# State space stage of a two-layer encoder step: scans of 512 columns instead of 128, and output products in fp32 over 128 rows

## The chip, the core and the metric

The kernel runs on one core of a Trainium2 chip. A core has five engines that each follow their own instruction order: TensorE (PE in the profile, with its weight loads as PEld), VectorE (DVE), ScalarE (ACT), GpSimd (POOL) and SyncE (SP, which here only issues DMAs). The metric is the device time of one execution in microseconds. Three runs of the kernel before gave 2142.64, 2145.76 and 2148.68 us, so the median is 2145.76 us.

## The reference

The program is one streaming step of a small encoder with two layers. Layer 0 mixes the sequence with a diagonal complex state space model (S5), layer 1 with a gated delta rule. Both are evaluated for a prompt of 2048 positions and for 8 short samples of 16 positions. The change touches layer 0 alone, and there the recurrence:

```python
# per group g of 16 channels, 64 complex states p
x_t = Abar * x_{t-1} + Bbar @ u_t          # complex, one decay per (g, p)
y_t = Re(C @ x_t)
y   = gelu(y + d * u);  y = y * sigmoid(y @ w_glu + b_glu) * silu(z)
out = y @ w_out
```

with `u, z = split(h @ w_in)`. The states after the last position are outputs too, of the prompt (`s5_re_prompt`, `s5_im_prompt`) and of the samples.

## The kernel before

Eight positions form one column. The 2048 prompt positions are 256 columns (`NPC`), the samples' 128 positions another 16, so every tile of the first layer has 272 columns (`NCH`). Layer 0 goes through three stages:

- Stage A computes the left half `u` of the input projection (`pd`), stores it, and builds tables: powers of `Abar` and the scaled `B` and `C` for 16 steps (`sp_d`), and rotation tables (`tw_d`).
- Stage B runs the state space model in 16 steps of four groups each (`s5_setup`, `s5_load`, `s5_main`). Between these instructions PE computes the right half `z` of the projection in 64 blocks (`z_block`, product `pdz`, 24 matmuls a block): each weight and activation is split into a high and a low part, and three products are summed (lines 150 to 152). The z blocks are written last in the program and have no deadline, so the scheduler takes them as filler for PE; only the last six carry an order (`later([ends...])`): they stand behind the output products of step 15.
- Stage C does the gate (`pg`, with `w_glu`) and the output projection (`po`, with `w_out`). Its weights come in blocks of 512 KB through two buffers (`wr`, pool `wrc`): DMA into `wgr` or `wor`, a cast on ACT into the high part (`wgh`, `woh`, L136), a subtraction on DVE for the low part (`wgl`, `wol`, L138). Eight blocks of `w_glu` are followed by eight of `w_out` and eight blocks `w2q` of the second layer.

One S5 step on its engines. Setup, one step ahead: four DVE products and a sum give `abt`, PE transposes it to `ab` (L679); four DVE products (L685, L686) and a difference (L687) give `ca`, which ACT and DVE split into a high and a low part (`cah`, `cal`, L130 and L131); PE makes the short-range kernel `pk` from it (L695), which goes through DRAM and comes back as `toe`. Main part: PE multiplies `u` by `ab` for the two pairs of groups, into `pb` (L732; PSUM has one buffer for it); ACT copies the sample columns (`bs`, L735); DVE rotates the prompt columns by the table (`f`, L737), adds and subtracts (`z`, L739 and L740), and scans: 256 columns in two segments of 128, for two pairs and for real and imaginary part apart, so eight scans of 128 columns (L746). Between the two segments four small DVE instructions (L750 to L753) rotate the end of the first into the start of the second. Two products rotate back (`t`, L760), a difference and a sum give the states `x` (named `xs` in the trace, L762 and L763). The 128 rows are two groups of 64 states. `x` is split into high and low parts (`xsh` on ACT, `xsl` on DVE). For each of four groups PE then sums `toe` times `u` in fp32 (L772) and six products over 64 rows (L777: real and imaginary part, each high by high, high by low, low by high), two groups side by side in the rows of the array. ACT applies gelu (L781), and the result goes to DRAM (`y_d`).

What sets the order: apart from the first part of stage A, which is written out by hand, the framework's scheduler fixes the instruction order of each engine when the program is built. On the chip each engine follows that order. SP and ACT issue the DMAs in their order as well, so a DMA that waits holds up the ones behind it. After its last loads for step 15, SP stores the samples' states (`s5s`, L800) and the prompt's states (`s5p`, L796), then loads the blocks of `w_glu` (L134), the outputs `y` (`yc`, L892) and `z` (`zt`, L931).

Beside DVE's last steps, POOL computes the samples' final states: eight tensor operations from L797 on, among them those of `advance`.

## Time and profile before

| | |
|---|---|
| median of three runs | 2145.76 us (2142.64 to 2148.68) |
| the profiled execution, its own time | 2142.89 us |
| its span, first to last instruction | 2141.1 us |
| busy in the span | PE 97%, DVE 73%, ACT 45%, POOL 23% |
| stage B, from the first `pdz` to the last | 270.7 to 617.8 us |
| mean granted PE clock | 0.989 |

The profile lists, for one execution, when every instruction started and how long it took. PE's matmuls are pipelined: one of 272 columns takes 0.29 us from start to end, but the next can start 0.13 us after it. An fp32 matmul stands in the trace as two records. A chain row names what set the time at that moment; a wait row names who waited for whom, the sum in us, how often, and the longest.

### The profile page before, as it was taken

What the parts mean: (1) busy time and instruction counts of PE and PEld (TensorE: products, weight loads), DVE (VectorE), ACT (ScalarE), POOL (GpSimd) and SP (SyncE); (2) the same over time, 40 slices, a digit from 0 to 9 for tenths busy, and PEclk for the clock granted to TensorE, in tenths of its full rate; (3) what the DMA queues carried; (4) which work ended last, traced back from release to release, by engine and by line L of the source; (5) the groups of instructions that cost most, each with busy time, mean ns of one, the idle gap of its engine ahead of it and who ended that gap; (6) DMA issues with size and microseconds to landing.
All of it is one profiled execution on the core that took longest, in us unless ns stands there. A gap on an engine that the chain in (4) does not pass through costs nothing.

```text
span 2141.1 us, 42274 instructions
## 1 busy us (share of the span) xinstructions
PE 2070.2 (97%) x15729; PEld 1832.9 (86%) x15729; DVE 1554.7 (73%) x4049; ACT 971.9 (45%) x2298; POOL 485.9 (23%) x720
## 2 busy tenths in 40 slices
PE   6899999999889999999999999999999799999998
PEld 4888888888689999999888879889987588888887
DVE  6979598999856555445665659697656788888885
ACT  3534333333245544445765432342223566666663
POOL 1267410000112322222100000100011244444430
PEclk9999999999889999999999999999999999999999
DMA  9787854454286533335566322654355944454432
GB/s 278 269 267 243 257 152 142 142 172 144 91 241 213 196 125 111 110 100 172 173 201 179 86 63 70 167 132 126 126 179 168 303 135 141 147 147 147 147 114 70
DMA packets 398666, 344.99 MB, mean 161 GB/s; under 512 B 88410, under 2 KB 359274, under 8 KB 398460
## 3 DMA queue, kind: packets, MB, share of 16 engines
q1 hardware_dynamic: 261388, 234.95, 36.9%
q10 hardware_dynamic: 134256, 99.69, 14.5%
q0 software_dynamic: 2816, 7.65, 1.0%
q8 instruction: 124, 2.03, 0.4%
q14 instruction: 82, 0.67, 0.1%
HBM read 221.40 MB, written 120.80 MB: 160 GB/s over the span
## 4 chain that ended last, share of the span: by engine, by line
PE 78%; DVE 10%; DMA 7%; ACT 2%; issue 1%; POOL 1%; SPq 0%; ACTq 0%; DVEq 0%; POOLq 0%
PE epo L69 7%; PE pc L150 6%; PE pc L152 5%; PE pc L151 5%; PE pz L152 3%; PE pz L151 3%; PE pz L150 3%; PE pdz L151 3%; PE pdz L150 3%; PE pdz L152 3%; PE po L150 2%; PE po L152 2%; PE po L151 2%; PE pg L152 2%; PE pg L150 2%; PE pg L151 2%
## 5 line engine op out<-in xcount | busy, mean ns | idle before, releaser
L150 PE MATMUL pc<-h1h,wdh 128*128 128x512 f32 (+1 forms) x600 | 216.5, 361 | 0.0
L151 PE MATMUL pc<-h1l,wdh 128*128 128x384 f32 (+1 forms) x600 | 214.8, 358 | 0.2 <-POOL h1l L1357 0.2
L152 PE MATMUL pc<-h1h,wdl 128*128 128x384 f32 (+1 forms) x600 | 214.9, 358 | 0.0
L1417 DVE SCALAR_TENSOR_TENSOR ac<-pb,convw,ac 128x384 f32<-128x384 f32 (+3 forms) x288 | 163.8, 593 | 3.3
L150 PE MATMUL pdz<-hhz,wzh 128*128 128x272 f32 x512 | 151.5, 297 | 2.1 <-ACT evz L627 2.1
L151 PE MATMUL pdz<-hlz,wzh 128*128 128x272 f32 x512 | 152.2, 297 | 0.0
L152 PE MATMUL pdz<-hhz,wzl 128*128 128x272 f32 x512 | 150.7, 295 | 0.0
L150 PE MATMUL po<-gh,woh 128*128 128x272 f32 x512 | 148.1, 290 | 2.7 <-ACT gh L942 2.7
L150 PE MATMUL pg<-yh,wgh 128*128 128x272 f32 x512 | 148.2, 289 | 1.9 <-ACT evz L627 1.9
L151 PE MATMUL pg<-yl,wgh 128*128 128x272 f32 x512 | 149.1, 291 | 0.0
L151 PE MATMUL po<-gl,woh 128*128 128x272 f32 x512 | 147.8, 289 | 0.5 <-DVE gl L942 0.4
L152 PE MATMUL pg<-yh,wgl 128*128 128x272 f32 x512 | 148.3, 290 | 0.0
L152 PE MATMUL po<-gh,wol 128*128 128x272 f32 x512 | 147.7, 289 | 0.0
L150 PEld LDWEIGHTS pc<-h1h,wdh 128*128 128x128 f32 x600 | 112.6, 188 | 12.2 <-issue 1.7
L151 PEld LDWEIGHTS pc<-h1l,wdh 128*128 128x128 f32 x600 | 112.7, 188 | 10.6 <-issue 0.8
L152 PEld LDWEIGHTS pc<-h1h,wdl 128*128 128x128 f32 x600 | 112.6, 188 | 10.2 <-issue 0.8
L150 PE MATMUL pd<-hh,wuh 128*128 128x272 f32 x384 | 112.5, 294 | 0.1
L69 PE MATMUL epo<-w2h,ohi 128*128 128x512 f32 x272 | 111.5, 410 | 0.0
L151 PE MATMUL pd<-hl,wuh 128*128 128x272 f32 x384 | 110.8, 289 | 0.3 <-DVE hl L231 0.3
L152 PE MATMUL pd<-hh,wul 128*128 128x272 f32 x384 | 110.8, 289 | 0.0
L939 POOL TENSOR_TENSOR zt<-zt,sz 128x272 f32<-128x272 f32 x64 | 63.1, 991 | 204.1 <-ACT sz L938 197.3
L69 PE MATMUL epo<-w2l,ohi 128*128 128x512 f32 x272 | 107.5, 395 | 1.9 <-DMA w2l<-w2l_d 1.8
(615 smaller groups left out, 6349.2 us busy)
## 6 DMA issues: line engine op xcount, KB each, us to landing
wa<-in_w_ada SPq DMA_DIRECT2D x32, 512.0 KB
wdr<-in_w_in SPq DMA_DIRECT2D x24, 512.0 KB
h_d<-x ACTq DMA_DIRECT2D x8, 1088.0 KB
u_d<-ev ACTq DMA_DIRECT2D x64, 136.0 KB
hz<-h_d SPq DMA_DIRECT2D x16, 544.0 KB
u<-u_d SPq DMA_DIRECT2D x16, 544.0 KB
z_d<-evz ACTq DMA_DIRECT2D x64, 136.0 KB
y_d<-y ACTq DMA_DIRECT2D x32, 272.0 KB
```

The costliest lines, as they stand in the source:

```text
L69: i_ = f(*a, **kw)
L150: T.matmul(ps, lhsT=w_hi[k], rhs=x_hi[k], start=(k == 0), stop=False)
L151: T.matmul(ps, lhsT=w_hi[k], rhs=x_lo[k], start=False, stop=False)
L152: i_ = T.matmul(ps, lhsT=w_lo[k], rhs=x_hi[k], start=False, stop=(k == n - 1))
L939: G.tensor_mul(zt, zt, sz)
L1417: V.scalar_tensor_tensor(o, src(j), convw[:, b, j:j + 1], o, op0=ALU.mult, op1=ALU.add)
```

## The change

The setup makes `ca` with two products of 576 columns instead of four of 288. The split of `ca` into two parts is gone: four ACT copies arrange it in a tile `cx` so that for each group the 64 real rows and the 64 imaginary rows lie one over the other in 128 rows. This moves half of the rows across partitions.

In the main part `z` is laid out by segment first, so that real and imaginary part and both pairs of one segment are 512 columns in a row. A tile `rr` (two buffers, filled once a step by an ACT copy) holds the decay in every column except the first of each 128, where it holds zero; so one scan of 512 columns does what four scans did, since a zero decay starts afresh. The carry from the first segment is added to the first column of the second by six small DVE instructions instead of four. DVE writes the states to a tile `xo`, and four ACT copies move them into `x`, again with real and imaginary rows over each other; four more ACT copies do this for the sample columns (`xh`). The split of `x` into high and low part is gone. PE sums for each group the fp32 product of `toe` and one fp32 product of `cx` and `x` over 128 rows (L791): four a step instead of 24 in the split form. POOL clears the two `rr` tiles once.

The scheduler orders the instructions anew. Three places matter for what follows. First PE, between step 14 and step 15 (`py14_0` is the output tile of the first group of step 14, `pb15_0` and `pb15_1` are the two input products of step 15). Before:

```order
L772 MATMUL py14_0_6136<-u14_5907,toe14_5948 128x272
L772 MATMUL py14_1_6137<-u14_5907,toe14_5948 128x272
L732 MATMUL pb15_0_6180<-u15_6041,ab15_6054 64x272 x4
L732 MATMUL pb15_1_6189<-u15_6041,ab15_6054 64x272 x4
L777 MATMUL py14_0_6136<-xsh14_6131,cah14_5934 128x272
L777 MATMUL py14_1_6137<-xsh14_6131,cah14_5934 128x272
```

With the change:

```order
L789 MATMUL py14_0_5874<-u14_5663,toe14_5703 128x272
L789 MATMUL py14_1_5875<-u14_5663,toe14_5703 128x272
L741 MATMUL pb15_0_5900<-u15_5778,ab15_5791 64x272 x4
L791 MATMUL py14_0_5874<-xs14_5825,cx14_5688 128x272
L791 MATMUL py14_1_5875<-xs14_5825,cx14_5688 128x272
L741 MATMUL pb15_1_5908<-u15_5778,ab15_5791 64x272 x4
```

The second input product of step 15 has moved behind the first two products over the states of step 14.

Second SP, just ahead of the first step (`wr1` are weight blocks of the z projection, `sp` the tables, `stN` the samples' states, `wgr` the blocks of `w_glu` for stage C):

```order
 L134 DMA wr1_7_4072<-in_w_in0 128x8x128
+L668 DMA sp_0_4123<-sp_d0_87 128x310
+L668 DMA sp_1_4172<-sp_d1_88 128x310
+L134 DMA wgr0_7950<-in_w_glu 128x8x128
+L134 DMA wgr1_7954<-in_w_glu 128x8x128
 L642 DMA stN_4106<-in_stN 128x512
```

Two blocks of `w_glu` have moved from behind the store of the prompt's states to before stage B; two more (`wgr2`, `wgr3`) stand after the last load of step 15, and the last four behind the first three loads of `yc`.

Third DVE in step 14, with the change (`wgl` is the low part of a weight block, `xo` the states):

```order
L774 TENSOR_TENSOR t14_5862<-z_5824,tw_14_5665 128x1024 x2
L138 TENSOR_TENSOR wgl0_7891<-wgr0_7950,wgh0_7890 128x1024
L777 TENSOR_TENSOR xo14_5865<-t14_5862 128x512
L778 TENSOR_TENSOR xo14_5865<-t14_5862 128x512
L138 TENSOR_TENSOR wgl1_7889<-wgr1_7954,wgh1_7888 128x1024
L745 TENSOR_TENSOR f15_5899<-pb15_0_5900,tw_15_5780 128x2x2x128 x2
```

Before, all eight `wgl` stood behind the last instruction of step 15.

```diff
@@ -658,6 +658,11 @@
 
         fe = b1.tile([P, 2, 32, 2], F32, name="fe")
 
+        halves = (slice(0, 64), slice(64, 128))
+        rrs = [b1.tile([P, 2, 2, SEG], F32, name=f"rr{i}") for i in range(2)]
+        for rr in rrs:
+            G.memset(rr, 0.0)
+
         def s5_setup(b):
             sp = b3.tile([P, SPW], F32, tag="sp", bufs=2, name=f"sp_{b}")
             nc.sync.dma_start(sp, sp_d[b])
@@ -681,13 +686,15 @@
 
             ca = b3.tile([P, 2, 2, 9, 16], F32, tag="ca", bufs=2, name=f"ca{b}")
             t2 = b1.tile([P, 2, 2, 9, 16], F32, tag="tt", name=f"cat{b}")
-            for l in range(2):
-                V.tensor_mul(ca[:, l], bc(bc(ccv[:, 0, l], 1, 9), 1, 2), bc(pw[:, l, 1:3], 3, 16))
-                V.tensor_mul(t2[:, l], bc(bc(ccv[:, 1, l], 1, 9), 1, 2), bc(pw[:, l, 0:2], 3, 16))
+            pn = sp[:, PWO:BBO].rearrange("p (l m) -> p l m", l=2)
+            for dst, r in ((ca, 0), (t2, 1)):
+                V.tensor_mul(dst.rearrange("p l r n c -> p l (r n) c"), bc(ccv[:, r], 2, 18),
+                             bc(pn[:, :, 9 - 9 * r:27 - 9 * r], 3, 16))
             V.tensor_sub(ca, ca, t2)
-            cs_ = [b2.tile([P, 2, 2, P], F32R, tag="ca" + i, name=f"ca{i}{b}") for i in "hl"]
-            split_w(*(t.rearrange("p l r (n c) -> p (l r) n c", c=16) for t in cs_),
-                    ca[:, :, :, 1:9].rearrange("p l r n c -> p (l r) n c"))
+            cx = b2.tile([P, 2, 2, P], F32, tag="cx", name=f"cx{b}")
+            for r in range(2):
+                for g2 in range(2):
+                    S.copy(cx[halves[r], :, g2].rearrange("p l (n c) -> p l n c", c=16), ca[halves[g2], :, r, 1:9])
 
             pk = ps_t.tile([P, P], F32, tag="t", name=f"pk{b}")
             for l in range(2):
@@ -703,7 +710,7 @@
             toe = b2.tile([P, 4, P], F32, tag="toe", name=f"toe{b}")
             for g in range(4):
                 nc.sync.dma_start(toe[:, g, :], dram_ap(k_d[b], 16 * g * 240, [[16, 8], [240, 16], [1, P]]))
-            return cs_, ab, toe
+            return cx, ab, toe
 
         def s5_load(b):
             u = b2.tile([P, 4, NCH], F32, tag="ur", name=f"u{b}")
@@ -713,69 +720,75 @@
             nc.sync.dma_start(tw, tw_d[b])
             return u, tw
 
-        def s5_main(b, u, tw, ca, ab, toe):
+        def s5_main(b, u, tw, cx, ab, toe):
             prs = slice(2 * b, 2 * b + 2)
-            z = b2.tile([P, 2, 2, NPC], F32, tag="z", name="z")
+            rr = rrs[b % 2]
+            S.copy(rr[:, :, :, 1:SEG], bc(bc(rN[:, prs], 1, 2), 3, SEG - 1))
+            z = b2.tile([P, 2, 2, 2, SEG], F32, tag="z", name="z")
             x = b2.tile([P, 2, 2, NCH], F32, tag="x", name=f"xs{b}")
-            xh = x[:, :, :, NPC:NCH].rearrange("p l r (q h) -> p l r q h", h=2)
+            xh = b2.tile([P, 2, 2, 8, 2], F32, tag="xh", name=f"xh{b}")
             G.memset(x[:, :, :, 0:1], 0.0)
             S.copy(xh[:, :, :, :, 0], stN[:, prs])
 
             def seg(a):
                 return a.rearrange("p r (s c) -> p r s c", s=2)
 
-            f = b2.tile([P, 2, 2, 2, NPC], F32, tag="f", name=f"f{b}")
+            f = b2.tile([P, 2, 2, 2, 2, SEG], F32, tag="f", name=f"f{b}")
             for pl in range(2):
                 pb_ = ps_b.tile([P, 2, 512], F32, tag="b", name=f"pb{b}_{pl}")
                 for ri in range(2):
                     for g2 in range(2):
                         T.matmul(pb_[64 * g2:64 * g2 + 64, ri, 0:NCH], lhsT=ab[:, 2 * pl + 1 - ri, 64 * g2:64 * g2 + 64],
                                  rhs=u[:, 2 * pl + g2], start=True, stop=True, tile_position=(0, 64 * g2))
-                bsv = bs[:, 2 * b + pl]
-                S.copy(bsv.rearrange("p r q h -> p r (q h)"), pb_[:, :, NPC:NCH])
+                S.copy(bs[:, 2 * b + pl].rearrange("p r q h -> p r (q h)"), pb_[:, :, NPC:NCH])
                 for i in range(2):
-                    V.tensor_mul(seg(f[:, i, pl]), seg(pb_[:, :, 0:NPC]), bc(bc(tw[:, pl, i], 1, 2), 1, 2))
-                V.tensor_add(xh[:, pl, :, :, 1], ax[:, 2 * b + pl], bsv[:, :, :, 0])
+                    V.tensor_mul(f[:, i, :, :, pl].rearrange("p s r c -> p r s c"), seg(pb_[:, :, 0:NPC]),
+                                 bc(bc(tw[:, pl, i], 1, 2), 1, 2))
             V.tensor_add(z[:, :, 0], f[:, 0, :, 0], f[:, 1, :, 1])
             V.tensor_sub(z[:, :, 1], f[:, 0, :, 1], f[:, 1, :, 0])
+            V.tensor_add(xh[:, :, :, :, 1].rearrange("p l r q -> p (l r) q"), ax[:, prs].rearrange("p l r q -> p (l r) q"),
+                         bs[:, prs, :, :, 0].rearrange("p l r q -> p (l r) q"))
+            for r, rl in enumerate(halves):
+                for g2, gl in enumerate(halves):
+                    S.copy(x[rl, :, g2, NPC:NCH], xh[gl, :, r].rearrange("p l q h -> p l (q h)"))
             cy = b2.tile([P, 3, 2, 2], F32, tag="cy", name="cy")
+            fl = "p r l c -> p (r l c)"
             for sg in range(2):
-                for pl in range(2):
-                    for ri in range(2):
-                        zs = z[:, pl, ri, sg * SEG:(sg + 1) * SEG]
-                        V.tensor_tensor_scan(zs, rN[:, 2 * b + pl:2 * b + pl + 1].broadcast_to([P, SEG]), zs,
-                                             cy[:, 0, pl, ri:ri + 1] if sg else 0.0, op0=ALU.mult, op1=ALU.add)
+                zs = z[:, sg].rearrange(fl)
+                V.tensor_tensor_scan(zs, rr.rearrange(fl), zs, 0.0, op0=ALU.mult, op1=ALU.add)
                 if sg == 0:
-                    ze = z[:, :, :, SEG - 1]
-                    V.tensor_mul(cy[:, 1], ze, bc(tw[:, :, 0, SEG - 1], 2, 2))
-                    V.tensor_mul(cy[:, 2], ze, bc(tw[:, :, 1, SEG - 1], 2, 2))
-                    V.tensor_sub(cy[:, 0, :, 0], cy[:, 1, :, 0], cy[:, 2, :, 1])
-                    V.tensor_add(cy[:, 0, :, 1], cy[:, 1, :, 1], cy[:, 2, :, 0])
+                    ze = cy[:, 0]
+                    z1 = z[:, 1, :, :, 0]
+                    V.tensor_mul(ze, z[:, 0, :, :, SEG - 1], bc(rN[:, prs], 1, 2))
+                    V.tensor_mul(cy[:, 1], ze, bc(tw[:, :, 0, SEG - 1], 1, 2))
+                    V.tensor_mul(cy[:, 2], ze, bc(tw[:, :, 1, SEG - 1], 1, 2))
+                    V.tensor_add(z1, z1, cy[:, 1])
+                    V.tensor_sub(z1[:, 0], z1[:, 0], cy[:, 2, 1])
+                    V.tensor_add(z1[:, 1], z1[:, 1], cy[:, 2, 0])
 
             def rs(a):
-                return a.rearrange("p l r (s c) -> p l (r s) c", s=2)
-
-            t = b2.tile([P, 2, 2, 2, NPC], F32, tag="f", name=f"t{b}")
+                return a.rearrange("p s r l c -> p (s r) l c")
+
+            t = b2.tile([P, 2, 2, 2, 2, SEG], F32, tag="f", name=f"t{b}")
             for i in range(2):
-                V.tensor_mul(rs(t[:, i]), rs(z), bc(tw[:, :, i], 2, 4))
-            m = NPC - 1
-            V.tensor_sub(x[:, :, 0, 1:NPC], t[:, 0, :, 0, 0:m], t[:, 1, :, 1, 0:m])
-            V.tensor_add(x[:, :, 1, 1:NPC], t[:, 0, :, 1, 0:m], t[:, 1, :, 0, 0:m])
-            S.copy(fe[:, :, prs], t[:, :, :, :, m])
-            xs = [b2.tile([P, 2, 2, NCH], F32R, tag="x" + i, name=f"xs{i}{b}") for i in "hl"]
-            split_w(*xs, x)
+                V.tensor_mul(rs(t[:, i]), rs(z), bc(tw[:, :, i], 1, 4))
+            xo = b1.tile([P, 2, 2, 2, SEG], F32, tag="xo", name=f"xo{b}")
+            ts = [t[:, i].rearrange("p s r l c -> p r l s c") for i in range(2)]
+            V.tensor_sub(xo[:, 0], ts[0][:, 0], ts[1][:, 1])
+            V.tensor_add(xo[:, 1], ts[0][:, 1], ts[1][:, 0])
+            S.copy(fe[:, :, prs], t[:, :, 1, :, :, SEG - 1].rearrange("p i r l -> p i l r"))
+            xf_ = xo.rearrange("p r l s c -> p r l (s c)")
+            for r, rl in enumerate(halves):
+                for g2, gl in enumerate(halves):
+                    S.copy(x[rl, :, g2, 1:NPC], xf_[gl, r, :, 0:NPC - 1])
             ends = []
             for pl in range(2):
                 y = b2.tile([P, 2, NCH], F32, tag="y", name=f"y{b}_{pl}")
                 pys = [ps_y.tile([P, NCH], F32, tag="y", name=f"py{b}_{2 * pl + i}") for i in range(2)]
                 for i in range(2):
                     T.matmul(pys[i], lhsT=toe[:, 2 * pl + i], rhs=u[:, 2 * pl + i], start=True, stop=False)
-                for r in range(2):
-                    for wi, xi in ((0, 0), (0, 1), (1, 0)):
-                        for i in range(2):
-                            ln = slice(64 * i, 64 * i + 64)
-                            i_ = T.matmul(pys[i], lhsT=ca[wi][ln, pl, r], rhs=xs[xi][ln, pl, r],
-                                          start=False, stop=(r == 1 and wi == 1), tile_position=(64 * i, 0))
+                for i in range(2):
+                    i_ = T.matmul(pys[i], lhsT=cx[:, pl, i], rhs=x[:, pl, i], start=False, stop=True)
                 ends.append(i_.ins)
                 for i in range(2):
                     S.activation(y[:, i, :], pys[i], AF.Gelu_apprx_tanh)
```

## Prediction

> **What bounds the kernel now.** I read the busy time by stretches first, then who PE waited for, then the chain of waits through the end of the state space stage. The stretches are its steady part, its end, and the part of stage C in which weights still arrive. Columns: busy us and instructions of PE, PEld, DVE, ACT and POOL, then granted clock, DMA share and GB/s.
>
> ```profile
> core 0: us, PE busy (x) PEld busy (x) DVE busy (x) ACT busy (x) POOL busy (x), PEclk, DMA share, GB/s
> 290.00:553.00 263.00, 262.81 (x2025) 219.61 (x2024) 241.81 (x515) 92.31 (x225) 4.02 (x27) 1.00 0.48 146
> 553.00:601.00 48.00, 36.62 (x206) 26.69 (x206) 34.16 (x57) 11.55 (x27) 8.44 (x9) 0.72 0.34 107
> ...
> 618.00:706.00 88.00, 82.94 (x631) 81.25 (x631) 58.72 (x106) 50.16 (x89) 23.72 (x23) 0.98 0.73 232
> ```
>
> For 263 us PE is never free. DVE is busy 242 of them, but PE does not feel it. PE's waits in 290 to 553 are the first row here (waiter, releaser, us in total, times, longest), the next two belong to 553 to 620, the last to 618 to 706:
>
> ```profile
> PE pb L732 <- DMA u<-u_d: 0.2, 1, 0.2
> ...
> PE py L777 <- ACT xsh L130: 6.5, 2, 5.2
> ...
> PE pdz L150 <- ACT evz L627: 2.1, 1, 2.1
> ...
> PE po L150 <- ACT gh L942: 2.7, 4, 1.3
> ```
>
> So up to 553 us only PE's own instructions set the pace, and DVE's time there is worth nothing. From 553 on the z blocks run short and steps 14 and 15 stand alone. The chain (start, us, what) shows what then sets the time:
>
> ```profile
> 560.91 1.29 DVE f L737 x2
> 562.28 0.64 DVE z L739
> ...
> 563.52 1.29 DVE z L746 x4
> ...
> 571.26 2.10 PE pb L732 x8
> ...
> 576.17 1.70 DVE z L739
> ...
> 578.91 2.97 DVE z L746 x4
> ...
> 585.47 2.37 DVE t L760 x2
> 587.86 0.69 DVE xs L762
> ...
> 589.38 0.34 SPq L796
> 589.78 4.65 DMA wgr<-in_w_glu
> ...
> 602.85 2.31 DMA y_d<-y
> ...
> 606.89 9.71 DMA wgr<-in_w_glu
> ...
> 698.27 5.39 DMA w2l_d<-w2q
> ```
>
> DVE carries 561 to 589; from 589 to some 704 the chain is the weight loads with their casts. They start when SP has stored s5p (589.38), and the fifth block on stands behind the store of the last y (602.85) and the loads of it. After that PE leads again. The change is worth what it moves in three places: PE's own time up to 553, the tail to 603, and the loads behind it.
>
> **PE's own time.** Prices from the chain: two fp32 products (four records), twelve split products, `pk`, `abT`, and the first `pb` of step 14. Below them the single starts around one visit of split products among z products.
>
> ```profile
> 526.09 0.92 PE py L772 x4
> 527.00 0.95 PE py L777 x12
> 527.96 0.57 PE pk L695 x8
> ...
> 533.45 0.59 PE abT L679 x4
> ...
> 553.14 1.07 PE pb L732 x8
> ```
>
> ```profile
> 442.20 0.29 PE L152 MATMUL pdz<-hhz,wzl 128*128 128x272 f32 x1
> 442.33 0.29 PE L150 MATMUL pdz<-hhz,wzh 128*128 128x272 f32 x1
> 442.55 0.39 PE L777 MATMUL py<-xsh,cah 64*128 64x272 f32 x2
> 442.87 0.39 PE L151 MATMUL pdz<-hlz,wzh 128*128 128x272 f32 x1
> ```
>
> z products start 0.13 us apart. Going into 64 rows takes 0.22, a pair and the way out 0.32; so a visit costs 0.09 + 0.19 = 0.28 beyond its work. A step has 12 pairs at 0.13 (1.5 us) and about three visits (0.84): 2.34 us. Four fp32 products at 0.46 are 1.84. That saves 0.5 us a step, 6.5 us over the 13 steps ahead of step 14. In the built order 1331 z products stand ahead of the first `pb` of step 14, where 1340 stood: 9 x 0.13 = 1.1 us off. Against it `pk` and `pb` are entered six times more often (cut up by single products), at some 0.2 us: 1.1 us on. So that `pb` moves from 553.1 to 546.6, if PE never waits.
>
> **Will it wait?** DVE and ACT, by form, in 280 to 605 us (count, busy, mean ns):
>
> ```profile
> L746 DVE TENSOR_TENSOR_SCAN z<-rN,cy,z 128x128 f32<-128x128 f32 x64 | 26.5, 468 | 0.0
> L746 DVE TENSOR_TENSOR_SCAN z<-rN,z 128x128 f32<-128x128 f32 x64 | 23.8, 429 | 0.0
> L131 DVE TENSOR_TENSOR xsl<-xs,xsh 128x1088 fp32r<-128x1088 f32 x16 | 20.6, 1286 | 1.6 <-ACT xsh L130 1.6
> L686 DVE TENSOR_TENSOR cat<-sp 128x288 f32<-128x288 f32 x30 | 12.4, 455 | 0.4
> L687 DVE TENSOR_TENSOR ca<-ca,cat 128x576 f32<-128x576 f32 x15 | 11.2, 748 | 0.2
> L131 DVE TENSOR_TENSOR cal<-ca,cah 128x512 fp32r<-128x512 f32 x15 | 10.2, 682 | 0.6 <-ACT cah L130 0.6
> L751 DVE TENSOR_TENSOR cy<-z,tw 128x4 f32<-128x4 f32 x16 | 2.5, 156 | 0.0
> ```
>
> ```profile
> L130 ACT CAST xsh<-xs 128x1088 fp32r<-128x1088 f32 x16 | 17.6, 1100 | 16.3 <-DVE xs L763 16.3
> L130 ACT CAST cah<-ca 128x512 fp32r<-128x512 f32 x15 | 9.3, 621 | 37.1 <-PE py L777 32.7 <-DVE z L746 3.5 <-DVE ca L687 0.9
> ```
>
> A scan of 512 columns isn't in the trace. Below it is bounded by a plain product of 512 columns (`cal`, 0.68), above by four scans (1.29 together in the chain, 4 x 0.47 by the mean). I take 1.2, near the four back to back; the work is the same column by column. DVE per step: scans 50.3/16 = 3.1 become 2.4; `xsl` (1.29) and `cal` (0.68) go; four products of 0.455 become two of 0.75 (0.3 off); two more small ones (0.3 on): 2.7 us less, 43 us in 16 steps, of which the 263 us above get nothing. If that cover went (some 12 us a step of z products), DVE would lead.
>
> ACT: two casts go (1.72). Their slope, (1100 - 621)/576 = 0.83 ns a column, gives 0.62 us for each copy of 510 columns of `x` and for `rr`, 0.41 for each of `cx`, 0.2 for the sample copies: 5 x 0.62 + 4 x 0.41 + 4 x 0.2 = 5.5. So 3.8 us more a step, on 92/263 of 19 us: about 10.5 of 19. No trace shows a copy across partitions; from nothing extra to double, I take the cast's price.
>
> The loop that PE waits on runs from the second `pb` to `x`: f 1.29, z twice 0.64, scan, six small and scan 3.4, t 2.37, x twice 0.69, three copies 1.9: 11.6 us. Setup work that the order puts between them adds up to 2.8 (two of `ca`'s form at 0.75, a split of the z input, of `xsl`'s shape): 11.6 to 14.4. PE's order leaves, between the second `pb` of step 10 and its first fp32 product over `x`, 78 z products (9.8 at 0.125), six fp32 products (2.8), `pk`, `abT` and a `pb` (2.2): 14.8 us. That just holds. I allow 1.5 us of waits and put `pb` of step 14 at 548, 5 us early; the waits lie between 0 and 20 (the slower rival).
>
> **The tail.** By the order shown with the change, the second `pb` of step 15 now stands behind products that need step 14's `x`, so the two steps no longer overlap there; and two weight blocks of stage C are loaded before stage B. These delay the first `u` by at most two loads of 4.65 us; PE has 92 z products (12 us) ahead of its first `pb`, where it had 71, so that is hidden. Their low halves on DVE (1.2 us each, near `xsl`'s shape) now stand in step 14, one of them ahead of `x`.
>
> From T, the first `pb` of step 14: 26 z products and two `pb` 5.5; the loop 11.6 and the weight half 1.2: `x` at T + 18.3, for which PE has waited some 4 us; fp32 pair and `pb` 2 to 4.5 with the clock down; the loop of step 15 without its copies 9.7: DVE's end at T + 31 undisturbed. POOL disturbs it, as it did:
>
> ```profile
> 575.12 2.21 POOL L797 TENSOR_TENSOR ax<-ax,bs 128x512 f32<-128x512 f32 x1 [19.83 <-DVE xs L738]
> ```
>
> Beside POOL's eight operations `z` took 1.70 where it took 0.64, four scans 2.97 where they took 1.29: with the small ones some 4 us. So DVE ends at T + 35, where it took 36 (s5p at 589.4 = 553.1 + 36.3). Copies 1.9, fp32 pair 1 to 2.4, 18 z products 2.3 to 4, four more fp32 1.84, gelu: the last y goes out at T + 46, where it was T + 49.7 (602.85): 3.7 us less.
>
> The Trainium skill, SBUF, section "SBUF: two separate sides", says that a DVE instruction with two SBUF inputs and a GpSimd one exclude each other for the whole instruction. By that a scan of 512 is held up once where four are held up four times, which by the rows above takes up to 1.7 us more off the tail: 2137 instead of 2139.
>
> **The loads.** Two blocks come early and two more in the tail, but the built SP order puts the other four behind the loads of y, where three stood. One load is 4.65 us alone, about half of it, 2.4, beside another; of the 3.7 us that leaves 1.3. Sum: 5 + 1.3 = 6.3 us, to 2134.8 us of span. This execution took 2142.89 - 2141.1 = 1.8 us beyond its span and lies 2.9 below the median: 2139.5, say 2139 us.
>
> **Rivals.** *The loads swallow it.* The chain to 704 is blocks in two buffers; if the four blocks behind y cost two full loads more (9.3 us), all is given back: 5 + 3.7 - 9.3, 2143 to 2147 us. For it: PE waits only 5 us in 618 to 706, so it cannot pass the loads. Against: two loads overlap. *The tail shrinks.* If x of step 14 meets PE without the 4 us wait, the clock stays up and POOL blocks less, y goes out at T + 38: 8 us more, 2131. *Slower.* The place is the first fp32 product of a step, the mechanism ACT's four copies in a queue that also empties z and y. It decides from 14.8 us of loop; a scan of 1.9 and copies at double price make it 11.6 + 1.4 + 1.9 = 14.9, with setup work up to 17.7. PE then waits about 1.5 us a step, 13 steps 20 us, less 6.3: 2159; half of it 2149. Against it stands that the nearest rows (`cal`, `cah`) put both pieces lower.
>
> The Trainium skill, TensorE: Matmul & The Clock Gate, section "What's actually happening", has PE at half rate after an idle window of some 3.4 us; the clock of 0.72 in 553 to 601 agrees. It speaks against the new tail, which has two such gaps.
>
> **Numbers.** A change of 0.3% (6.4 us) is about what a measurement of this kernel can tell from none. Forecast 0.50, own range 2134 to 2143, a bit over half of it past the bound; tail shrinks 0.18; loads swallow it 0.18; slower 0.14. Faster 0.27 + 0.18 = 0.45, within 0.23 + 0.18 = 0.41, slower 0.14. The range runs from 2127 (the short tail with PE's full 6.5) to 2154 (waits between half and full).
>
> **What will show it.** PE's waits on ACT's copies in the steady part: under 3 us in all, or I am wrong on the loop. The start of step 14's `pb` at 545 to 550; the scan's mean between 1.1 and 1.3 us; the second `pb` of step 15 behind a PE wait of about 4 us; the chain from 590 to 700 still made of weight loads, with its end 4 to 8 us earlier. A scan above 1.6 us, or `pb` of step 14 later than 553, makes the prediction wrong; so does a chain without loads.

## The result, and the profile after

The change takes 2132.7 us (median of five runs, 2131.31 to 2134.16), the kernel before 2142.64 us over five runs (2140.57 to 2148.68). The ratio is 0.9945, 95% interval 0.9931 to 0.996: about 0.5% faster. Beside the experiments it was timed once more: 2133.34 us, ratio 0.9963, 0.995 to 0.9977. The profiled execution took 2134.16 us, its span is 2132.4 us, 8.7 less than before.

The same views as in the prediction, now of the change. Busy time by stretches (columns as before: PE, PEld, DVE, ACT, POOL busy, granted clock, DMA share, GB/s):

```profile
290.00:546.00 256.00, 255.80 (x1786) 215.93 (x1781) 213.76 (x395) 143.38 (x371) 3.84 (x27) 1.00 0.49 150
547.00:591.00 44.00, 28.23 (x161) 22.23 (x161) 31.86 (x46) 21.40 (x49) 9.92 (x9) 0.84 0.36 113
...
633.00:700.00 67.00, 62.64 (x472) 61.02 (x471) 45.16 (x85) 38.68 (x69) 19.22 (x19) 0.97 0.70 226
```

PE is still never free up to 546 us; DVE, with 241.8 of 263 us before, now has 213.8 of 256, and ACT went from 92.3 to 143.4. In the end of the stage PE idles more than before (28 busy of 44 us), but at a clock of 0.84 instead of 0.72. PE's waits in 285 to 546 (one row), 546 to 612 and 608 to 700 us (waiter, releaser, us in total, times, longest):

```profile
PE abT L684 <- ACT kp L707: 0.3, 1, 0.3
...
PE py L791 <- ACT xs L783: 14.2, 2, 11.6
PE pg L150 <- ACT evz L627: 2.8, 1, 2.8
PE py L789 <- ACT y L794: 1.0, 1, 1.0
...
PE po L150 <- ACT gh L955: 2.8, 4, 1.5
```

No wait in the steady part is for a copy of `x`. The chain of waits through the end of the stage (start, us, what):

```profile
547.08 1.07 PE pb L741 x8
551.61 1.07 PE pb L741 x8
...
564.50 0.62 ACT xs L783
565.26 1.27 PE py L791 x4
566.53 1.09 PE pb L741 x8
...
569.88 1.70 DVE z L748
571.60 1.54 DVE z L758
...
575.58 1.24 DVE z L758
576.83 3.79 DVE t L774 x2
580.65 0.70 DVE xo L777
...
583.40 2.15 PE py L791 x4
...
591.02 2.04 DMA y_d<-y
...
594.17 6.68 DMA wgr<-in_w_glu
...
688.75 5.18 DMA w2l_d<-w2q
```

It has the shape of before: steps 14 and 15 alone, then weight loads to some 694 us. The groups of DVE and ACT, by form, in 280 to 605 us (count, busy, mean ns, idle before):

```profile
L758 DVE TENSOR_TENSOR_SCAN z<-rr,z 128x512 f32<-128x512 f32 x32 | 39.4, 1231 | 0.9
...
L783 ACT COPY xs<-xo 64x510 f32<-64x510 f32 x64 | 39.5, 617 | 15.2 <-DVE xo L777 13.7 <-ACT evz L627 0.4
```

The scan of 512 columns takes 1.23 us, a copy of `x` across partitions 0.62 us.

Where the 8.7 us of span lie, from the first start of each product in the two traces (`pdz`, `pb` of step 14, last `py`, `pg`, `pc`):

| stretch | before | after | difference |
|---|---|---|---|
| start to first `pdz` | 270.7 | 268.4 | -2.3 |
| to first `pb` of step 14 | 282.4 | 278.6 | -3.7 |
| to the last `py` of step 15 | 47.1 | 43.2 | -3.9 |
| to the first `pg` | 19.8 | 19.0 | -0.9 |
| to the first `pc` | 396.2 | 397.3 | +1.1 |
| to the end | 1125.0 | 1126.1 | +1.0 |

The last row bounds what one execution can tell: the change doesn't touch that stretch, and in the profiles shown here it lay between 1124.7 and 1128.8 us.

### The profile page after: what moved, and what is told of

It reads as the page before. It is cut to its first block, busy times and chain, and to the rows that moved or that the text cites. A ratio compares the mean times of both kernels' runs of the same rounds, so it can differ in the third digit from the quotient of the medians.

```text
span 2132.4 us, 41793 instructions
## 1 busy us (share of the span) xinstructions
PE 2058.8 (97%) x15473; PEld 1829.6 (86%) x15473; DVE 1524.1 (71%) x3905; ACT 1035.7 (49%) x2474; POOL 484.5 (23%) x722
## 4 chain that ended last, share of the span: by engine, by line
PE 71%; DVE 5%; DMA 5%; ACT 3%; issue 1%; SPq 0%; POOL 0%; ACTq 0%; DVEq 0%; POOLq 0%
PE epo L69 7%; PE pc L150 5%; PE pc L151 5%; PE pc L152 5%; PE pz L152 3%; PE pz L151 3%; PE pz L150 3%; PE po L150 2%; PE po L152 2%; PE po L151 2%; PE pdz L150 2%; PE pdz L152 2%; PE pdz L151 2%; PE pg L152 2%; PE pg L150 2%; PE pg L151 2%
```

## Experiments

All are timed against the kernel before, run beside them; it took 2141.45 to 2144.80 us there, so between experiments the ratios compare better than the times. In one table (the change in its two timings first); "dealt" and "paced" are explained below.

| kernel | median us | ratio to before, 95% | last `py` minus first `pb` of step 14 |
|---|---|---|---|
| the change | 2132.7 | 0.9945 (0.9931 to 0.996) | 43.2 |
| the change again | 2133.34 | 0.9963 (0.995 to 0.9977) | 46.0 |
| wide scans alone | 2144.44 | 0.9999 (0.9986 to 1.0012) | 43.1 |
| eight short scans | 2149.73 | 1.0022 (1.0013 to 1.0032) | 43.8 |
| short scans, z held | 2151.12 | 1.0045 (1.0031 to 1.0058) | 48.8 |
| short scans, z dealt | 2135.54 | 0.9954 (0.9938 to 0.997) | 43.7 |
| POOL late | 2132.1 | 0.9937 (0.9922 to 0.9953) | 40.8 |
| z held for the tail | 2133.27 | 0.9942 (0.9928 to 0.9957) | 49.9 |
| no preload | 2133.16 | 0.9965 (0.9952 to 0.9979) | 44.3 |
| paced z, empty start | 2130.83 | 0.995 (0.9936 to 0.9964) | 42.9 |
| paced z, full start | 2120.09 | 0.989 (0.9875 to 0.9906) | 40.7 |
| paced z, POOL early | 2124.59 | 0.991 (0.9895 to 0.9925) | 46.2 |
| before, paced z | 2129.14 | 0.9931 (0.9916 to 0.9945) | 38.6 |

### The change again

Without an edit, beside "no preload", "short scans, z held" and the first paced version.

> The change itself, to have it beside the others on one chip: 2131 to 2135 us; first pdz at 268.4 us, within 0.6, if the 2.3 us ahead of stage B come from the order and not from chance.

2133.34 us, first `pdz` at 268.28: as expected. Its tail, 2.8 us longer than in the first profile, comes back below.

### Wide scans alone

The products over `x` go back to the split form, the scans stay at 512 columns.

```diff
-                for i in range(2):
-                    i_ = T.matmul(pys[i], lhsT=cx[:, pl, i], rhs=x[:, pl, i], start=False, stop=True)
+                for r in range(2):
+                    for wi, xi in ((0, 0), (0, 1), (1, 0)):
+                        for i in range(2):
+                            ln = slice(64 * i, 64 * i + 64)
+                            i_ = T.matmul(pys[i], lhsT=ca[wi][ln, pl, r], rhs=xs[xi][ln, pl, r],
+                                          start=False, stop=(r == 1 and wi == 1), tile_position=(64 * i, 0))
```

> The kernel before with the wide scans alone: z by segment, rr, two scans of 512 columns a step; the products over x stay in the split form over 64 rows, with x built in place and split as before (x itself in one buffer instead of two, for space). By my theory PE sets the pace of the steady part and the scans only matter in the tail: first pdz and the first pb of step 14 stay where they were before (270.7 and 553 us, within 1.5), the tail from there to the last y is 1 to 3 us shorter than before (49.7 us), and the time is 2138 to 2142 us (before 2142.6, with the whole change 2132.7). Rival (the gain is the scans): DVE's relief moves pb of step 14 to about 547, and the time is 2132 to 2135 us.

The time is that of the kernel before. The stretches from the first `pdz` to step 14, and from there to the last `py`, of this kernel:

```profile
276.62:559.08 282.46, 282.46 (x2181) 238.04 (x2179) 259.25 (x493) 106.68 (x257) 10.55 (x39) 1.00 0.48 147
559.08:602.13 43.05, 33.04 (x195) 24.10 (x195) 30.24 (x51) 9.54 (x24) 10.04 (x9) 0.76 0.37 114
```

and of the kernel before:

```profile
270.69:553.07 282.38, 282.19 (x2180) 236.77 (x2178) 260.40 (x550) 98.42 (x241) 9.67 (x37) 1.00 0.48 148
553.07:600.12 47.05, 35.67 (x201) 25.96 (x200) 34.09 (x57) 11.48 (x27) 8.44 (x9) 0.71 0.32 102
```

The steady part is the same to 0.1 us: there the scans are worth nothing, as I had it, and the change's 3.7 us come with the other part. The tail is 4 us shorter; the time is not. From the last `py` to the first `po` this execution took 48.1 us where the kernel before took 45.5, and its stage A took 6 us longer (PE waits 3.8 us for DVE there instead of 1.9). Whether that is this execution or this kernel's order the run doesn't tell. My 2138 to 2142 was too low.

### Eight short scans

The other half: fp32 products and copies stay, the scans are four of 128 columns a segment again.

```diff
-                zs = z[:, sg].rearrange(fl)
-                V.tensor_tensor_scan(zs, rr.rearrange(fl), zs, 0.0, op0=ALU.mult, op1=ALU.add)
+                for pl in range(2):
+                    for ri in range(2):
+                        zs = z[:, sg, ri, pl]
+                        V.tensor_tensor_scan(zs, rN[:, 2 * b + pl:2 * b + pl + 1].broadcast_to([P, SEG]), zs, 0.0,
+                                             op0=ALU.mult, op1=ALU.add)
```

> The whole change but for the scans: four scans of 128 columns for each of 512, straight from the decay, without rr. By my theory eight scans cost PE nothing in the steady part: PE waits there stay under 2 us, and the first pb of step 14 is late only by the z products that the new order puts ahead of it (1392 instead of 1331, so 61 x 0.125 = 7.6 us: 554 to 556 us instead of 547). In the tail the scans come back on the chain, with fewer z products (144 instead of 205) to fill it: the time is 2133 to 2140 us. Rival (the wide scans carry the steady part): pb of step 14 later than 558 us with PE waiting for copies of x, and the time is above 2141 us.

It is 17 us slower than the change and slower than the kernel before, beyond what I had expected. The order tells more than the waits. z products ahead of the first `pb` of some steps, as built:

```
step                     6     10     12     13     14
before                 653   1001   1172   1243   1340
the change             654   1010   1164   1248   1331
eight short scans      694   1118   1320   1389   1392
```

The order with short scans hands out its filler early. On the chip `pb` of step 14 starts at 564.4 us: 61 more products are 7.6 us, and then nothing is left. From 546 to 565 us PE is busy 9.7 of 19 us. So the run doesn't yet tell whether a step with short scans is longer, or only the order worse.

### Short scans, the filler held, then dealt out

First the last blocks were held back, as `later` does for the last six already:

```diff
-            with later([ends[zst["n"] > 58]] if zst["n"] > 57 else []):
+            n = zst["n"]
+            with later([ends[2]] if n > 58 else [ends[1]] if n > 57 else [ends[0]] if n >= 57 else [pre] if n >= 55 else []):
```

(`ends` now begins with the last `pb` of the step, `pre` is that of the step before.)

> As the run with eight short scans, but with z blocks 55 and 56 held behind the second pb of step 14 and block 57 behind the second pb of step 15, so that about as many z products are left for the tail as in the change (216 against 205; 1320 ahead of step 14 against 1331). Theory: that run lost because the order spent its z products early, not because short scans slow the steady part. Then the first pb of step 14 is at 546 to 549 us, the tail to the last y is 1 to 5 us longer than in the change (43.2 us), and the time is 2133 to 2138 us. Rival (short scans cost the steady part): pb of step 14 later than 551 us and the time is above 2141 us.

By its numbers the rival won: `pb` of step 14 at 557.4 us, the time 2151. But the stretches say how:

```profile
268.09:526.98 258.89, 258.44 (x1869) 224.72 (x1869) 211.02 (x452) 130.92 (x339) 8.99 (x31) 1.00 0.50 151
526.98:557.36 30.38, 18.57 (x85) 10.62 (x85) 24.53 (x58) 14.28 (x42) 0.40 (x3) 0.78 0.35 107
```

Up to step 12 PE has 0.5 us without work; 1320 z products are then used up, and in steps 12 and 13, for which none was held, PE waits. Holding the last blocks only moves the bare stretch forward. So all blocks were dealt out, with the steps' own pace:

```diff
-            with later([ends[zst["n"] > 58]] if zst["n"] > 57 else []):
+            n = zst["n"]
+            st = int((n - 7) / 3.6)
+            with later([ends[1 + (n > 58)]] if n > 57 else [pbs[min(st, 15)]] if st >= 0 else []):
```

(`pbs[k]` is the last `pb` of step k.)

> Eight short scans with the fp32 products once more, now with the z blocks dealt out as in the change: block n waits for the second pb of step (n - 7)/3.6, which puts 1330 z products ahead of step 14 (1331 in the change) and 653, 991 and 1157 ahead of steps 6, 10 and 12 (654, 1010, 1164). In the two runs before, the order had spent 1320 z products by step 12, and the last steps stood bare. Theory (the loss lay in the order): first pb of step 14 at 546 to 549 us, the tail 1 to 5 us longer than in the change, time 2133 to 2138 us. Rival (a step with short scans is longer than PE's work, 18.6 us): PE waits in the steady part, pb of step 14 later than 552 us, time above 2141 us.

```profile
268.40:546.99 278.59, 275.77 (x1961) 235.69 (x1959) 232.96 (x506) 144.44 (x379) 9.08 (x34) 1.00 0.49 150
546.99:590.72 43.73, 29.61 (x157) 23.16 (x157) 33.88 (x60) 20.99 (x49) 7.50 (x9) 0.80 0.38 114
```

`pb` of step 14 at 546.99 us, where the change has it at 547.01; tail 43.7; 2135.5 us. The ratio's interval covers the change's. So at the change's own pace of some 18.6 us a step eight short scans cost the steady part nothing that shows (PE is idle 2.8 us in it, 0.5 in the change), and the wide scans are worth at most the 2 to 3 us between the medians, which this measurement can't tell from none. What the wide scans did was to let the order keep its filler: without them, and in the scheduler's own order, the same products lose 17 us. Why the scheduler spends it early with short scans is not shown; I only see the order. Nor was it tried whether short scans would also keep up with the shorter steps of the paced versions below.

### POOL's last operations behind DVE's end

```diff
+        G.tensor_copy(stN[:, 0, 0, 0:2], fsp[:, 0])
+        G.tensor_add(stN[:, 0, 0, 0:2], ax[:, 0, 0, 0:2], bs[:, 0, 0, 0:2, 0])
         G.tensor_add(ax, ax, bs[:, :, :, :, 0])
...
-        nc.sync.dma_start(O["s5s"], stN)
+        nc.gpsimd.dma_start(O["s5s"], stN)
```

> The whole change, with POOL's final state operations made to wait for DVE's last result (a copy of fsp ahead of them), and the store of the states on POOL's own queue so that no load waits for it. Theory POOL: beside POOL z took 1.70 instead of 0.64 us, t 3.79 instead of 2.37; without it DVE's end comes 2 to 3.5 us earlier than 581.4, and the time is 2129.5 to 2131 us. Rival (the slow instructions were slowed by something else, the writes of weights or ACT): z and t stay slow and the time stays within 1 us of 2132.7.

DVE's last step without POOL beside it, instruction by instruction (start, us, engine, line):

```profile
570.94 0.69 DVE L748 TENSOR_TENSOR z<-f 128x512 f32<-128x512 f32 x1
571.66 1.22 DVE L758 TENSOR_TENSOR_SCAN z<-rr,z 128x512 f32<-128x512 f32 x1
...
575.04 2.36 DVE L774 TENSOR_TENSOR t<-z,tw 128x1024 f32<-128x1024 f32 x2
```

Against the chain above `z` takes 0.69 instead of 1.70 us, the first scan 1.22 instead of 1.54, the pair of `t` 2.36 instead of 3.79: POOL it is, and the rival falls. From the start of `z` (L748) to the end of `t` DVE takes 6.5 us here and 10.8 in both profiles of the change: beside POOL it loses 4.3 us. DVE's last instruction starts 32.5 us after `pb` of step 14 instead of 35.0 (37.0 in the change's second profile). The 2.5 us against the first profile are less than 4.3 because here the second `pb` of step 15 ran at half rate (2.08 instead of 1.14 us), as it did in the second profile, and DVE's `f` behind it started some 2 us later. In the time it can't be told apart: 2132.1 beside 2132.7 and 2133.3 us.

### z products held for the tail

Blocks 53 and 54 go behind the second `pb` of step 14, 55 to 57 behind that of step 15, in the change itself:

```diff
-            with later([ends[zst["n"] > 58]] if zst["n"] > 57 else []):
+            n = zst["n"]
+            with later([ends[2]] if n > 58 else [ends[1]] if n > 57 else [ends[0]] if n >= 55 else [pre] if n >= 53 else []):
```

> The whole change, with five z blocks held back: two go behind the second pb of step 14, three behind the second pb of step 15 (1272 z products ahead of step 14 instead of 1331, 72 instead of 0 between the last pb and the first product over x of step 15). Theory: the tail's loss is PE standing idle for x (3.0 and 11.6 us). If the held blocks fill that, the waits on copies of x in the tail fall from 15 to 3 to 7 us, the last y goes out 5 to 9 us earlier and the time is 2124 to 2128 us. Rival (the load chain to 690 us sets the end, not PE): PE waits only move behind 610 us, and the time is 2130 to 2134 us. Third: the order changes elsewhere and takes it back, 2133 or more.

`pb` of step 14 came at 540.9 us, 6.1 earlier, and the last `py` at 590.8, no earlier. Two pieces of the chain show why:

```profile
539.82 1.24 DVE z L758
541.12 1.11 issue
542.22 1.22 DVE t L774
543.44 1.21 DVE f L745 x2
544.79 2.08 PE pb L741 x8
...
555.39 0.47 PE py L789 x2
555.88 3.98 DMA u<-u_d
559.99 1.14 PE pb L741 x8
```

When step 14 begins, DVE is still at step 13's scans and `t`; `f` of step 14 waits for it, and PE with it (the `pb` at half rate, 2.08 us). Still, the first scan of step 14 starts at 550.7 us, 4.9 earlier than in the change, and PE's products over its `x` 4.1 earlier. This is lost again at step 15. SP loads its `u` when PE is through with step 13's `toe` products, and in front of the last of these now stand 39 z products behind the second `pb` of step 14, where 20 stood: they start at 555.5 us, 1.8 earlier than in the change, and so the `pb` of step 15 comes at 560.0, only 1.5 earlier. A split of the z input of 1.6 us, which the order now puts between DVE's scans of step 15, takes that too: the last instruction on the states (`xo`) starts at 581.0 us, only 0.3 earlier than in the change. So the held products stood in the way of the last step. Each theory of mine that looked only at PE's two waits was wrong here.

### No preload of `w_glu`

```diff
-            load_w(wg_hi[k], wg_lo[k], col_block(I["w_glu"], k),
-                   wr.tile([P, KC, P], F32, tag="r", name=f"wgr{k}"))
+            with later([si.ins]):
+                load_w(wg_hi[k], wg_lo[k], col_block(I["w_glu"], k),
+                       wr.tile([P, KC, P], F32, tag="r", name=f"wgr{k}"))
```

(`si` is the store of `s5p`.)

> The whole change, with all blocks of w_glu loaded behind the store of s5p, as in the kernel before; PE's order stays, only five z products move behind the third product of step 15. Theory of the loads: the early blocks save the w_glu chain about two casts of 2.4 us (in the change the eighth cast of w_glu ends 29 us after DVE's end, counted with two that lie before it), so without them the first pg comes 2 to 5 us later than in the change (609.1 us) although DVE's end comes up to 2 us earlier (no low half of a weight in step 14's loop), and the time is 2134 to 2138 us. Rival (the early blocks give nothing, since the chain is held up by the loads of y): first pg within 1 us, time within 1.5 us of the change.

First `pg` at 610.25 us, where the change has 609.1 and 611.2 in its two profiles; 2133.16 us beside 2133.34. The rival holds: where the first blocks are loaded is worth nothing that shows. Behind the last `py` PE still has 121 to 126 z products, some 15 us at 0.125, to run before `pg`.

### Paced z: all steps shorter

What is held for two steps alone stands in the way of the step behind them; so next all steps were to come earlier. The z blocks of the change, with POOL late, were dealt out at 3.6 blocks a step:

```diff
-            with later([ends[zst["n"] > 58]] if zst["n"] > 57 else []):
+            n = zst["n"]
+            st = int((n - 2) / 3.6)
+            with later([ends[1 + (n > 58)]] if n > 57 else [pbs[min(st, 15)]] if st >= 0 else []):
```

> The change with POOL's last operations behind DVE's end, and the z blocks dealt out evenly: block n waits for the second pb of step (n - 2)/3.6, so that 1241 z products stand ahead of step 14 instead of 1331 and the rest fill the tail. Theory: the tail is paced by the loops of steps 13 to 15 on DVE and ACT, so holding z only there gave nothing; with all steps some 0.8 us shorter the loops start 11 us earlier, the held products fill PE's waits, the last y is 6 to 12 us earlier than in the change, and the time is 2120 to 2128 us. Rival: the loop of DVE and ACT does not fit into a step of 18 us, PE then waits in the steady part, and the time is 2131 us or more.

2130.8 us, 2 to 3 us below the change and not the 2120 to 2128 expected. The tail did its part (PE busy 39 of 43 us), but the start was bare: with two free blocks PE waited 8.0 us ahead of step 0. With seven free blocks and 3.2 a step:

```diff
-            st = int((n - 2) / 3.6)
+            st = int((n - 7) / 3.2)
```

> The paced order again, without its empty start (PE had waited 8.0 us ahead of step 0, since only two z blocks were free there): seven blocks are free, then block n waits for the second pb of step (n - 7)/3.2; 1248 z products ahead of step 14. POOL's last operations behind DVE's end as in the paced run before. Theory (PE's waits in the tail are the loss that is left): pb of step 14 at 535 to 539 us, waits on copies of x in the tail under 5 us, last y at 578 to 584 us, time 2119 to 2126 us. Rival (the loops of DVE and ACT take more than the 17.5 us that are left for a step): PE waits in the steady part take it back, 2128 to 2134 us.

```profile
268.55:535.97 267.42, 263.24 (x1879) 224.77 (x1878) 231.46 (x425) 153.57 (x396) 9.54 (x34) 1.00 0.52 158
535.97:576.64 40.67, 38.02 (x244) 32.61 (x244) 25.09 (x43) 20.40 (x49) 7.84 (x11) 0.96 0.36 118
```

```profile
PE py L791 <- ACT xs L783: 2.6, 1, 2.6
```

2120.1 us: 1.1% below the kernel before, 12 to 13 us below the change. POOL's late operations are in this version too; what they are worth in it the next run tells. Step 14 begins at 536 us, PE waits 2.6 us for `x` in the tail where it waited 14.2, and the clock there is 0.96 instead of 0.84. This version beats both kernels. That the loops of DVE and ACT alone pace the tail, as the theory has it, is not shown by it: in the run with z held they started earlier as well. With POOL's operations back beside DVE's last step:

```diff
-        G.tensor_copy(stN[:, 0, 0, 0:2], fsp[:, 0])
-        G.tensor_add(stN[:, 0, 0, 0:2], ax[:, 0, 0, 0:2], bs[:, 0, 0, 0:2, 0])
         G.tensor_add(ax, ax, bs[:, :, :, :, 0])
...
-        nc.gpsimd.dma_start(O["s5s"], stN)
+        nc.sync.dma_start(O["s5s"], stN)
```

> The paced change with POOL's last operations left where the change has them, beside DVE's last step. Theory POOL: z and t of step 15 take 1.7 and 3.8 instead of 0.7 and 2.4 us again, DVE's end comes 2 to 3.5 us later than in the paced run (568.0), and the time is 1 to 3.5 us above 2120. Rival: other work covers it, the time is within 1 us of 2120.

```profile
536.84:583.04 46.20, 39.19 (x244) 33.66 (x244) 29.46 (x43) 20.47 (x49) 9.96 (x9) 0.89 0.37 122
```

```profile
565.72 1.76 DVE L758 TENSOR_TENSOR_SCAN z<-rr,z 128x512 f32<-128x512 f32 x1
567.52 3.26 DVE L774 TENSOR_TENSOR t<-z,tw 128x1024 f32<-128x1024 f32 x2
```

2124.6 us, 4.5 more; DVE's end comes 36.4 us after `pb` of step 14 instead of 32.1. It is a little more than I allowed (3.5). The two medians are from different timings and their intervals just overlap, so the size is less sure than the sign. Without POOL's part, then, dealing out the filler is worth 8 to 9 us to the change.

Last, the kernel before in the same dress, with POOL late (the edit shown there) and dealt at 3.2 blocks a step:

```diff
-            with later([ends[zst["n"] > 58]] if zst["n"] > 57 else []):
+            n = zst["n"]
+            st = int((n - 7) / 3.2)
+            with later([ends[1 + (n > 58)]] if n > 57 else [pbs[min(st, 15)]] if st >= 0 else []):
```

> The kernel before, with the z blocks dealt out as in the paced change (block n waits for the second pb of step (n - 7)/3.2; 1242 z products ahead of step 14 instead of 1340) and POOL's last operations behind DVE's end. It shows what the change is worth once the filler is dealt out. DVE is busy 242 of 263 us in the steady part before, some 17.4 us a step, where the change leaves 15.8. Theory (the change's saving of PE time and the filler add up): pb of step 14 at 541 to 544 us, time 2128 to 2134 us, so the change is worth 8 to 13 us in the paced form too. Rival (DVE's load before does not allow shorter steps): PE waits for f and x in the steady part by more than 5 us and the time is 2135 us or more. Third (dealing out alone does it): 2118 to 2124 us.

```profile
271.59:547.81 276.22, 270.52 (x2082) 225.22 (x2080) 260.89 (x551) 95.96 (x237) 9.61 (x38) 0.99 0.49 149
547.81:586.40 38.59, 38.30 (x297) 32.22 (x297) 27.07 (x54) 10.78 (x27) 7.85 (x11) 1.00 0.38 120
```

2129.1 us, where the kernel before took 2143.85 beside it: the filler and POOL are worth some 15 us to it, more than the change is. The change keeps its 9 us on top (2120.1). Here DVE's load does show: step 14 begins at 547.8 instead of the 541 to 544 that I expected, with 5.7 us in which PE had nothing to do and DVE busy 261 of 276 us; what the steady part lost the tail made good.

## Why the prediction was right or wrong

The forecast was 2139 us, 0.45 for faster; the time is 2132.7 us, faster by 0.55%. The sign holds, and the time lies in the whole range of 2127 to 2154 us; it lies 1.3 us below the forecast's own 2134 to 2143, and nearest to the rival with the short tail (2131). The gain was 9.9 us by the medians of five runs, 8.7 by the spans, and the sum had 6.3. The forecast lies 6.3 us above the time as well, but 3 of these are no term of the sum: I placed the profiled execution 2.9 us below the median, and over five runs that median is 2142.64, what the profiled execution took (2142.89).

**What was not in the sum: stage A, 2.3 us.** In the kernel before, SP fetches the first tables ahead of the weights of z, so DVE does its products of `ca` (L685) for steps 0 and 1 within stage A, from 115 us on; later PE waits for DVE's `modT`. The row of before, PE's waits in 180 to 270 us:

```profile
PE ada L187 <- DVE modT L197: 1.6, 1, 1.6
```

In the change this wait, 1.6 of the 2.3 us, is gone. In ten of the profiles with fp32 products `pdz` starts at 267.8 to 268.8 us (in the paced one with the empty start it was held on purpose); in the three with split products at 270.7, 271.6 and 276.6. That the order of the tables is the cause is read from the traces, not tried, and it isn't the whole: with wide scans alone DVE begins these products at 116 us as well, and stage B starts another 5.9 us later than in the kernel before. I had read the SP order around the tables and looked only at what the moved weight blocks would do.

**PE's own time: the right moment, in part by luck.** `pb` of step 14 was to come at 548, 5 us early; it came at 547.0, but 2.3 of the 6.1 belong to stage A, so stage B gave 3.7, and two terms of its sum were wrong by more than that. Adding up, over the trace from the first `pdz` to that `pb`, the time from each PE start to the next by product:

| us (count) | z | fp32 `toe` | over `x` | `pb` | `pk` | `abT` |
|---|---|---|---|---|---|---|
| before | 182.4 (1340) | 25.0 | 27.3 (312) | 32.3 | 9.1 | 6.4 |
| change | 186.5 (1330) | 22.5 | 18.6 (104) | 32.9 | 11.6 | 6.3 |

The products of `y` (those over `x` of 13 steps, `toe` of 14 but for one pair) fell by 11.2 us, some 0.85 a step; I had 0.5. But "six more narrow-tile entries, 1.1 us" was far too little: z is entered 104 times instead of 88, and 10 fewer z products cost 4.1 us more, where 10 x 0.125 less was due; with `pk` and `pb` that is 8.4 us. Fewer and fatter products of `y` are scattered singly through z, and each cut costs: by these numbers some 0.33 us for each of the 16 entries more. I had counted only the cuts by `pk` and `pb`. The term for waits, 1.5 us, measured 0.5.

**Would PE wait? No.** The scan (1.2 taken, 1.23 measured), the copies of `x` (0.62, 0.62), of `cx` (0.41, 0.40), the loop that fits (no wait on `xs` in the steady part): these steps hold, and the slower rival falls with them. At this pace DVE's saving was worth nothing there, as the run with wide scans alone and the dealt short scans show.

**The tail.** `x` of step 14 was to reach PE at T + 18.3 (it did at T + 18.2), DVE was to end at T + 35 (its last instruction starts at T + 35.0), the last y to go out at T + 46 (T + 43.9), where T is the first `pb` of step 14. The POOL term, some 4 us, is borne out by the 4.3 of the run with POOL late; I had put it on `z`, the scans and the small instructions, and 1.4 of it came at `t`. So the tail is 5.8 us shorter than before by the store of y in this profile, where I had 3.7. In the change's second profile the tail to the last `py` is 46.0 instead of 43.2 us, so 3.7 lies between the two. The term that was too large is the one behind DVE's end: from the store of the prompt's states to that of the last y it took 8.9 us, where I had 11 and the kernel before 13.5. Not foreseen was that PE waits 14.2 us for `x` instead of 6.5 and the tail is shorter all the same. I read this from what is left to run at the low clock: 27.4 us busy at 0.84 instead of 35.7 at 0.71; no run tries it apart. The two gaps that spoke against this tail are there (2.6 and 11.6 us); in this profile the granted clock fell behind the second alone (1.00 in 566 to 570 us, 0.70 in 582 to 591).

The sentence on the Trainium skill's SBUF page, section "SBUF: two separate sides" (a DVE instruction with two SBUF inputs and a GpSimd one that reads SBUF exclude each other for the whole instruction), gave a wide scan that is held up once. The trace agrees as far as that: one scan 1.54 instead of 1.22 us, where four short ones took 2.97 instead of 1.29. The 2 us that this was to take off the time didn't come: the 1.4 us saved at the scans came back at `t`, 3.79 us where it had taken 2.37 before, with POOL already done.

**The loads.** The step "blocks behind y cost 2.4 us" isn't borne out. From the last `py` to the end the kernel before takes 1541.0 us, the change 1542.3 and 1540.9 in its two profiles, and without preload it is 1541.3 and the time stays. (Without preload some blocks still stand behind the loads of y, so that price alone was not tried.) By my reading only the place where the chain of waits runs has moved: PE is busy most of that time with z products and the first `pg`, so chain and PE are about equally late. The rival "the loads swallow it" falls, since the gain was not given back. The rival "the tail shrinks" names nearly the right time (2131), but by a mechanism that didn't come: PE's wait grew.

**What the prediction didn't ask** is the larger thing: what sets the tail. I took the order's filler as given. The paced versions show that 13 to 15 us lay there for either kernel with POOL's part, more than in the change; for the change 8 to 9 of them are the filler's alone.

## What to carry to other kernels

Where a scheduler fills PE's gaps with independent work, count in the built order how much of it stands ahead of each step: a change of one engine's instructions can empty it early (17 us here, with hardly a wait up to 546 us) and dealing it out evenly can be worth as much as the change itself. Here shorter products paid only as far as they stayed together; a product cut in singly costs on its way in and out. And before a stall is filled, look at what the filler will stand in front of: in the last two steps alone it held up the load for the step behind, and gave nothing.

## What the runs showed of the hardware

The same order, with nearly the same wait, left PE once at full and once at half rate. The change's profile and its second one, single PE rows with the wait before them in brackets:

```profile
565.26 1.27 PE L791 MATMUL py<-xs,cx 128*128 128x272 f32 x4 [2.63 <-ACT xs L783]
566.46 1.14 PE L741 MATMUL pb<-u,ab 128*64 128x272 f32 x8
```

```profile
564.88 2.15 PE L791 MATMUL py<-xs,cx 128*128 128x272 f32 x4 [2.49 <-ACT xs L783]
566.97 2.08 PE L741 MATMUL pb<-u,ab 128*64 128x272 f32 x8
```

After 2.63 us the four records took 1.27 us, after 2.49 us 2.15, and the `pb` behind them 1.14 and 2.08; the granted clock in 566 to 570 us is 1.00 and 0.50. DVE's `f` behind that `pb` starts 20.9 and 22.9 us after the first `pb` of step 14: 2 of the 2.8 us between the two tails. With POOL late the wait at this place was 2.49 us too, and the four records took 2.15. The Trainium skill, TensorE: Matmul & The Clock Gate, section "What's actually happening", says that the activity window of some 3.4 us runs free of the kernel; the two rows agree with that, though no run here shows the window itself.

A zero decay in the scan's first column starts it afresh at no price that shows: 512 columns in 1.23 us, against 1.29 for four of 128 back to back. The copy that moves 64 rows to the other half of the partitions costs no more than one that stays: the 64 copies of `x`, half of which cross, all took 613 to 623 ns, and the slope of the casts had given 0.62 us.
